# One hybrid block on one core: the splits of the output projection's rows go through a ring of two slots, wider evictions of the values, decay scans and linear-attention groups placed later

## The chip, the cores and the metric

The kernel runs on one core of a Trainium2 chip. The core has a matrix engine (PE, TensorE, with its weight loads shown as PEld), a vector engine (DVE), a scalar engine (ACT), a general engine (POOL, GpSimd) and a queue for transfers (SP), each with an instruction stream of its own that it works off in order. Weights and activations come from DRAM into the on-chip memory SBUF, matmuls write to the banks of PSUM, and DVE or ACT empty these. The metric is the device time of one execution in microseconds (us), as the median of the runs. Lower is better.

## The reference

One block over x with 1024 tokens (T) of width 1024 (D), in float32:

```
h = rmsnorm(x) ; z = h @ w_in      # columns split among three mixers
pool: trailing means over 2, 4, 8, 16 tokens minus u, 64-wide linear per group
gla:  4 heads of 64, chunks of 64: b = cumsum(log_sigmoid(a) / 16) in a chunk
      o = (q e^(b-ref)) (k e^(ref-b))^T v  [causal]  +  (q e^b) S
      S = e^(b_last) S + (k e^(b_last-b))^T v ; rmsnorm per head, times silu(g)
fox:  8 heads of 64, F = cumsum(log_sigmoid(f)), softmax(q k^T / 8 + F_t - F_s) v
y = x + concat(pool, gla, fox) @ w_o
y = y + (silu(rms(y) w_gate) * (rms(y) w_up)) @ w_down ; final rmsnorm
```

Float32 accuracy of products is reached by splitting: each operand is a rounded high part and a low part (value minus high part), and a product is three matmuls, high by high, high by low and low by high.

## The kernel before

The kernel first normalizes x by blocks of 128 tokens, turns them (`norm_T`) to hT in high and low parts, and meanwhile multiplies by the columns for the values of linear attention and the small logits (`psg`). Then follow, in program order: the decays, the inputs of the pool mixer (`pool_in`), linear attention in two pairs of heads A and B (class `Gla`), forgetting attention (values in `fox_values`, queries and keys in `fox_qk`, four pairs of heads in `fox_attend`), the output projection, and the FFN.

*Projections.* `project` loads a column block of the weights, splits it (ACT the high part, DVE or POOL the low part, lines 118 and 119) and runs 48 matmuls of 128x512: two halves of the tokens, each into one of the two PSUM banks "gm" (zgk0p, zgq0p and zgg0p are the banks of keys, queries and gate of pair A, with a 1 for pair B; zp0p and zp1p those of the pool mixer's u; zq.p and zk.p those of attention). ACT or DVE empty a bank into gk, gq, sg or u, and the next but one half can begin only when its bank is empty. Between the matmuls of a projection, PE works through small groups that the call hands over (the lists `smalls`): `turn_keys` (transposes, banks pk), `state` (pkv), `within` (pat), `outputs` (po) and `turned` (pot). These depend on the decay factors d, eq and bc, which POOL, ACT and DVE make from two scans (la into bc).

*Splits of w_o.* `keep_wo(k)` loads block k of w_o (128 rows), splits it into high and low part and stores both in a scratch tensor in DRAM (`wod`), from where the output projection fetches them much later. Before, its eight calls stand behind `fox_values(0)`, with raw, high and low part each in a general slot G. Its rows are wos0 to wos7, with r, h and l behind.

*Memory.* G slots are 33 general tiles of 128x1024, handed out in the order in which they came free. Beside them are rings of the same tiles: "fb" has two slots, used by the squares of the norm (n1sq) and later by the forget sums of a pair of heads, "pp" three and "p" six. A new tile of a ring waits until all use of the slot's last tile is over.

*Values.* `fox_values(q)` makes the values of two pairs of heads for eight token blocks. Each block leaves a bank psv of 128x256, which ACT (high part, line 528) and DVE (low part, 529) empty, once for each of the two pairs of heads.

*Order.* The program is recorded in its order and then put in another by a scheduler of the compiler, which works with times it estimates itself. So where a row stands on an engine is taken from the built program.

Of the kernel before, what the change touches and what calls it, by code (L numbers as in the profile page):

```python
# [18 lines left out]
P = 128  # L19
# [12 lines left out]
def tile_hybrid_block(ctx: ExitStack, tc, x, w_fv, w_gv, w_zt, w_o, w_gu, w_down, ln, w_pool, w_a3, chans, b_f, consts, out):  # L32
# [23 lines left out]
    def free(*names):  # L56
        for n in names:
            idle.append(where.pop(n))

    def R(name, dtype=F32, tag="p"):  # L60

        i = rings[tag].pop(0)
        rings[tag].append(i)
        return big.tile([P, 1024], dtype, tag=f"g{i}", name=name)
# [4 lines left out]
    def f(ap):  # L69
        return ap.bitcast(F32)  # L70
# [207 lines left out]

    def keep_wo(k):

        hi, lo = load_g(w_o[k * P:(k + 1) * P, :], f"wos{k}", tag="G")
        SP.dma_start(wod[k, :, 0], f(hi))
        SP.dma_start(wod[k, :, 1], f(lo))
        free(f"wos{k}h", f"wos{k}l")

    def fetch_wo(k):
        hl = G(f"wo{k}h", F32R), G(f"wo{k}l", F32R)
# [9 lines left out]
    reset = G("reset")  # L297
    DVE.memset(reset, 1.0)
    DVE.memset(e3(reset)[:, :, 0:1], 0.0)
    bcs = []  # L300

    def decays():

        las = []
        for j in range(2):
            la = R(f"la{j}")
            for c in range(2):
                csl = slice(c * 512, c * 512 + 512)
                ps = PS("s", f"pla{j}_{c}")
                PE.matmul(ps, wa[:, j * P:(j + 1) * P], aT[0:48, csl], start=True, stop=True)  # L310
                DVE.tensor_scalar(out=la[:, csl], in0=ps, scalar1=ch[:, 2 + j:3 + j], scalar2=None, op0=ALU.add)
            las.append(la)
        lft = R("lft")
        log_sigmoid([(la, la, R(f"lat{j}", tag="pp")) for j, la in enumerate(las)] + [(fx[0:8], fx[0:8], lft[0:8])])
        for j, la in enumerate(las):
            bc = G(f"bc{j}")
            DVE.tensor_tensor_scan(out=bc, data0=reset, data1=la, initial=0.0, op0=ALU.mult, op1=ALU.add)
            bcs.append(bc)
        ones, Fc = R("ones"), R("Fc")
        DVE.memset(ones[0:8], 1.0)  # L320
        DVE.tensor_tensor_scan(out=Fc[0:8], data0=ones[0:8], data1=fx[0:8], initial=0.0, op0=ALU.mult, op1=ALU.add)
        SP.dma_start(Fd, Fc[0:8])
        free("fx")
# [192 lines left out]

    def fox_values(q, smalls=((),) * NT):

        V = [[G(f"v{2 * q + j}_{i}", F32R).rearrange("p (t h s e) -> p t h s e", t=4, h=2, s=2) for i in range(2)] for j in range(2)]
        ws = [load_w(w_fv[:, q, i * 1024:(i + 1) * 1024], f"wfv{q}_{i}", eng=POOL) for i in range(2)]  # L520
        for tb in range(NT):
            ps = PS("gm", f"psv{q}_{tb}")
            woven(ps[:, 0:256], [(tok(hT, k, tb), tuple(w_[:, (k % 4) * 256:(k % 4) * 256 + 256] for w_ in ws[k // 4]))
                                 for k in range(NK)], smalls[tb])
            for j in range(2):
                v_ = V[j][tb // 4][:, tb % 4]
                pv = ps[:, 128 * j:128 * j + 128].rearrange("p (h e) -> p h e", h=2)
                ACT.activation(v_[:, :, 0], pv, AF.Copy)
                DVE.tensor_tensor(out=v_[:, :, 1], in0=pv, in1=f(v_[:, :, 0]), op=ALU.subtract)
        return V  # L530

    def fox_qk(p):
# [16 lines left out]
    def fox_item(p, a, m, ops, fb, V, Y):  # L549
# [44 lines left out]
        for n in range(m + 1):  # L594
# [10 lines left out]
            for b in range(2):  # L605
                kb = 2 * n + b
                o0 = cut * b
                v_ = V[p % 2][kb // 4][:, kb % 4, a]
                ph = pp[:, 256 * b:512 - o0] if b else pp[:, 0:256]
                pl = pp[:, 768:1024 - o0] if b else pp[:, 512:768]  # L610
                both = (o[:, o0:256], v_.rearrange("p s e -> p (s e)"), ph)
                high = (o[0:64, o0:256], v_[:, 0], pl)
                last = kb == 2 * m + 1
                for n_, args in enumerate((high, both) if last else (both, high)):
                    PE.matmul(*args, start=(kb == 0 and n_ == 0), stop=(last and n_ == 1))  # L615
# [41 lines left out]
            gemm(ps, [((t_[:, 0, o0:o0 + P], t_[:, 1, o0:o0 + P]), (wh[:, ns], wl[:, ns])) for t_, (wh, wl) in zip(mixes, ws)])  # L657
            DVE.tensor_tensor(out=x2[:, ns], in0=ps, in1=x2[:, ns], op=ALU.add)

    decays()  # L660
    free("aT", "reset", "wa")
    us = [pool_in(j) for j in range(2)]
    A = Gla(0)
    A.keys()
    A.queries(((), A.turn_keys()))
    pools = pool_tile(1, us[1]), pool_tile(0, us[0])
    A.gates((A.state(), pools[0] + A.within(0)))
    B = Gla(1)
    B.keys((A.within(1) + A.outputs(0), A.outputs(1) + A.turned(0)))
    B.queries((A.turned(1) + pools[1], B.turn_keys()))  # L670
    free("misc")
    B.gates((B.state(), B.within(0)))
    o_ = [B.outputs(0), B.outputs(1)]
    V = fox_values(0, (B.within(1), o_[0][:1], o_[0][1:], o_[1][:1], o_[1][1:] + B.turned(0), B.turned(1), (), ()))
    for k in range(8):
        keep_wo(k)
    ops = fox_qk(0)
    free("gv0", "gv1", "attb0", "attb1")
    for p in range(4):
# [1 line left out]
            last_mix += [G(f"mix7_{g}", F32R).rearrange("p (h t) -> p h t", h=2) for g in range(2)]  # L681
        Y = G(f"y{p}") if p < 3 else None
        fox_attend(p, ops, V, Y)
        done = [f"{n}{p}_{a}" for n in ("q", "k", "kl") for a in range(2)] + [f"v{p}_{i}" for i in range(2)]
        if p == 1:
            V = fox_values(1)
            free(*[done.pop() for _ in range(2)])
        if p < 3:
            ops = fox_qk(p + 1)
        if p == 2:  # L690
# [432 lines left out]
```

## Time and profile before

| | |
|---|---|
| runs | 1179.23, 1176.51, 1177.58 us; median 1177.58 |
| profiled execution | 1175.42 us, span 1173.7 us, mean clock of PE 0.992 |
| instructions in the span | 15953 |
| norm, mixers, values up to attention's first scores | about 0 to 230 us |
| attention, values of the other half | to about 360 us |
| output projection, then FFN from about 520 us | the rest |
| read from HBM, written to HBM | 105.09 MB, 44.34 MB |

The span runs from the first to the last instruction of the execution; the time holds 1.7 us around it. A row of the timeline gives start and duration of an instruction (or of some alike, "x4", from the first start to the last end), its engine, line, operation, what it writes and reads, and in brackets how long the engine was idle before and what released it. Matmuls overlap, so their starts, and not their durations, show the pace. A row of a DMA issue ends with the time from issue to landing.

### The profile page before, as it was taken

The numbers are of one execution on the slowest core, as the hardware profiler recorded it, in microseconds if no ns is written. First come the engines' busy times: TensorE is split into PE (matmuls) and PEld (weight loads), VectorE is DVE, ScalarE is ACT, GpSimd is POOL, SyncE is SP. The second block draws the span as 40 slices with busy tenths as digits, with TensorE's granted clock in tenths as the row PEclk, the third lists the DMA queues.
The fourth block names the chain that finished last, engine by engine and source line by source line (L and its number), as shares of the span: only waits on it lengthen the run. The fifth ranks groups of instructions, "written<-read, shape, count | busy, mean of one in ns | idle before, by whom it ended". The sixth has DMA issues, their size and how long they took to land.

```text
span 1173.7 us, 15953 instructions
## 1 busy us (share of the span) xinstructions
PE 1136.0 (97%) x5928; PEld 958.5 (82%) x5928; DVE 828.2 (71%) x1365; ACT 536.0 (46%) x970; POOL 340.4 (29%) x260
## 2 busy tenths in 40 slices
PE   6999998999999999998999999999999999999996
PEld 5877878889978888886888888888888888888875
DVE  6697364387746866579997767767686685876686
ACT  6454233466654644456453433444344344334345
POOL 2231123343322413210302221022201370660784
PEclk9999999999999999999999999999999999999999
DMA  7121184411203734431323332242314688333233
GB/s 250 37 73 52 59 295 174 176 39 35 91 18 126 305 132 159 173 112 46 117 86 129 101 115 88 101 134 82 135 54 152 224 322 293 103 95 102 86 112 143
DMA packets 57692, 150.45 MB, mean 128 GB/s; under 512 B 5080, under 2 KB 5512, under 8 KB 57616
## 3 DMA queue, kind: packets, MB, share of 16 engines
q1 hardware_dynamic: 57184, 147.87, 36.5%
q0 software_dynamic: 432, 1.57, 0.4%
q8 instruction: 46, 0.75, 0.3%
q14 instruction: 30, 0.25, 0.1%
HBM read 105.09 MB, written 44.34 MB: 127 GB/s over the span
## 4 chain that ended last, share of the span: by engine, by line
PE 76%; DVE 4%; DMA 1%; issue 1%; POOL 1%; ACT 1%; SPq 0%; POOLq 0%; DVEq 0%; ACTq 0%
PE m L774 36%; PE d L1030 15%; PE pxa L144 4%; PE pxb L144 3%; PE o L615 3%; PE pt L601 2%; PE psv L152 2%; PE s L575 1%; PE s L576 1%; PE zq3p L152 1%; PE zq0p L152 1%; PE zq2p L152 1%; PE zk1p L152 1%; PE zk2p L152 1%; PE zk0p L152 1%
## 5 line engine op out<-in xcount | busy, mean ns | idle before, releaser
L774 PE MATMUL m<-hA_0h,wr 128*128 128x512 f32 x616 | 214.7, 391 | 1.2 <-ACT hr L729 1.2
L774 PE MATMUL m<-hA_1h,wr 128*128 128x512 f32 x616 | 214.9, 389 | 0.0
L774 PEld LDWEIGHTS m<-hA_0h,wr 128*128 128x128 f32 x616 | 116.1, 189 | 25.8 <-ACT hr L729 1.6
L774 PEld LDWEIGHTS m<-hA_1h,wr 128*128 128x128 f32 x616 | 115.8, 188 | 24.2
L1030 PE MATMUL d<-lw,ha 128*128 128x512 f32 x308 | 119.9, 389 | 0.9 <-DVE lw L880 0.9
L774 PE MATMUL m<-hA_0l,wr 128*128 128x512 f32 x308 | 120.3, 391 | 0.0
L774 PE MATMUL m<-hA_1l,wr 128*128 128x512 f32 x308 | 119.9, 389 | 0.0
L1030 PE MATMUL d<-hw,ha 128*128 128x512 f32 x308 | 119.3, 389 | 0.0
L1030 PE MATMUL d<-hw,la 128*128 128x512 f32 x308 | 118.4, 389 | 0.0
L756 ACT ACTIVATE wr<-ws 128x512 fp32r<-128x512 f32 x110 | 69.5, 632 | 101.5 <-DVE ws L755 50.1
L826 POOL TENSOR_TENSOR cg<-cu,cu 128x512 f32<-128x512 f32 x11 | 19.7, 1795 | 302.8 <-DVE cu L803 266.7
L757 DVE TENSOR_TENSOR wr<-ws,wr 128x512 fp32r<-128x512 f32 x110 | 76.8, 704 | 20.6 <-ACT wr L756 20.5
L880 DVE TENSOR_TENSOR la<-ra,ha 128x1024 fp32r<-128x1024 f32 (+1 forms) x42 | 57.2, 1368 | 32.0 <-ACT ha L879 24.7
L590 POOL TENSOR_TENSOR pb<-pb,rl 128x128 f32<-128x128 f32 (+3 forms) x32 | 39.0, 1222 | 117.5 <-DVE rl L587 108.9
L872 POOL TENSOR_TENSOR rw<-wd,wd 128x512 f32<-128x512 f32 x33 | 59.0, 1815 | 47.7 <-PE d L1030 47.6
L879 ACT ACTIVATE ha<-ra 128x1024 fp32r<-128x1024 f32 (+1 forms) x42 | 41.3, 987 | 65.6 <-DMA ra<-cd 56.8
L1030 PEld LDWEIGHTS d<-lw,ha 128*128 128x128 f32 x308 | 57.8, 188 | 13.3 <-DVE lw L880 1.3
L604 DVE TENSOR_TENSOR pp<-pt,pp 128x512 fp32r<-128x512 f32 (+1 forms) x80 | 50.2, 631 | 25.7 <-ACT pp L603 25.3
L774 PEld LDWEIGHTS m<-hA_0l,wr 128*128 128x128 f32 x308 | 58.1, 189 | 12.0
L774 PEld LDWEIGHTS m<-hA_1l,wr 128*128 128x128 f32 x308 | 58.0, 188 | 12.0
L1030 PEld LDWEIGHTS d<-hw,la 128*128 128x128 f32 x308 | 57.8, 188 | 12.1
L1030 PEld LDWEIGHTS d<-hw,ha 128*128 128x128 f32 x308 | 57.8, 188 | 11.9
(398 smaller groups left out, 2690.6 us busy)
## 6 DMA issues: line engine op xcount, KB each, us to landing
ra<-cd SPq DMA_DIRECT2D x35, 512.0 KB, 3.9
wu<-in_w_gu_dram SPq DMA_DIRECT2D x22, 512.0 KB, 4.6
wg<-in_w_gu_dram SPq DMA_DIRECT2D x22, 512.0 KB, 3.7
wd<-in_w_down_dram SPq DMA_DIRECT2D x22, 512.0 KB, 6.4
mix<-mixs SPq DMA_DIRECT2D x14, 512.0 KB, 5.3
cd<-cg SPq DMA_DIRECT2D x11, 512.0 KB, 6.3
cd<-cs SPq DMA_DIRECT2D x11, 512.0 KB, 3.4
cd<-cu SPq DMA_DIRECT2D x11, 512.0 KB, 3.3
```

The source lines that it names most:

```text
L144: PE.matmul(ps, a, b, start=(n == 0), stop=(n == last))
L152: PE.matmul(ps, a, b, start=(i == 0 and n == 0), stop=(i == len(terms) - 1 and n == 2))
L590: POOL.tensor_tensor(out=pb[:, 0:W], in0=pb[:, 0:W], in1=rl[:, 0:1].broadcast_to([P, W]), op=ALU.mult)
L604: DVE.tensor_tensor(out=pp[:, 512:512 + w], in0=pt[:, 0:w], in1=f(pp[:, 0:w]), op=ALU.subtract)
L615: PE.matmul(*args, start=(kb == 0 and n_ == 0), stop=(last and n_ == 1))
L756: ACT.activation(hi, src, AF.Copy)
L757: DVE.tensor_tensor(out=lo, in0=src, in1=f(hi), op=ALU.subtract)
L774: PE.matmul(ps, a, b, start=(n == 0), stop=(n == 11))
L872: POOL.tensor_tensor(out=raw_[:, j * 512:j * 512 + 512], in0=wd[h0, j0 + j][:, e0, :], in1=wd[h1, j0 + j][:, e1, :], op=op)
L879: ACT.activation(hi[:, sl], src, AF.Copy)
L880: DVE.tensor_tensor(out=lo[:, sl], in0=src, in1=f(hi[:, sl]), op=ALU.subtract)
L1030: PE.matmul(banks[t], a[:, o], b[:, ns], start=(j0 + j == 0 and m == 0), stop=(j0 + j == NF // 2 - 1 and m == 2))
```

## The change

`keep_wo` takes two slots of the ring "fb", one for the raw block and one for its high part; the low part is made in place over the raw block. Its eight calls now stand in pairs between the projections of linear attention. The decays are made in three pieces (`decay_logits`, `decay_sums` for each pair, `forget_sums`), the second pair's and the forget sums' later than before. The groups of linear attention are handed to a later projection each. `fox_values` keeps the values of both pairs of heads of two token blocks in one tile, and empties a bank with one ACT and one DVE operation.

```
     def keep_wo(k):
 
-        hi, lo = load_g(w_o[k * P:(k + 1) * P, :], f"wos{k}", tag="G")
+        raw, hi = R(f"wos{k}", tag="fb"), R(f"wosh{k}", F32R, tag="fb")
+        SP.dma_start(raw, w_o[k * P:(k + 1) * P, :])
+        ACT.activation(hi, raw, AF.Copy)
+        DVE.tensor_tensor(out=raw, in0=raw, in1=f(hi), op=ALU.subtract)
         SP.dma_start(wod[k, :, 0], f(hi))
-        SP.dma_start(wod[k, :, 1], f(lo))
-        free(f"wos{k}h", f"wos{k}l")
+        SP.dma_start(wod[k, :, 1], raw)
 
...
-    bcs = []
-
-    def decays():
-
-        las = []
+    las, bcs = [], []
+
+    def decay_logits():
         for j in range(2):
-            la = R(f"la{j}")
+            la = G(f"la{j}")
             for c in range(2):
...
             las.append(la)
-        lft = R("lft")
-        log_sigmoid([(la, la, R(f"lat{j}", tag="pp")) for j, la in enumerate(las)] + [(fx[0:8], fx[0:8], lft[0:8])])
-        for j, la in enumerate(las):
-            bc = G(f"bc{j}")
-            DVE.tensor_tensor_scan(out=bc, data0=reset, data1=la, initial=0.0, op0=ALU.mult, op1=ALU.add)
-            bcs.append(bc)
-        ones, Fc = R("ones"), R("Fc")
+
+    def decay_sums(j):
+
+        la = las[j]
+        log_sigmoid([(la, la, R(f"lat{j}", tag="pp"))])
+        bc = G(f"bc{j}")
+        DVE.tensor_tensor_scan(out=bc, data0=reset, data1=la, initial=0.0, op0=ALU.mult, op1=ALU.add)
+        bcs.append(bc)
+        free(f"la{j}")
+
+    def forget_sums():
+        lft, ones, Fc = (R(n, tag="pp") for n in ("lft", "ones", "Fc"))
+        log_sigmoid([(fx[0:8], fx[0:8], lft[0:8])])
         DVE.memset(ones[0:8], 1.0)
         DVE.tensor_tensor_scan(out=Fc[0:8], data0=ones[0:8], data1=fx[0:8], initial=0.0, op0=ALU.mult, op1=ALU.add)
         SP.dma_start(Fd, Fc[0:8])
...
 
     def fox_values(q, smalls=((),) * NT):
 
-        V = [[G(f"v{2 * q + j}_{i}", F32R).rearrange("p (t h s e) -> p t h s e", t=4, h=2, s=2) for i in range(2)] for j in range(2)]
+        V = [G(f"v{q}_{i}", F32R).rearrange("p (t j h s e) -> p t j h s e", t=2, j=2, h=2, s=2) for i in range(4)]
         ws = [load_w(w_fv[:, q, i * 1024:(i + 1) * 1024], f"wfv{q}_{i}", eng=POOL) for i in range(2)]
         for tb in range(NT):
             ps = PS("gm", f"psv{q}_{tb}")
...
-            for j in range(2):
-                v_ = V[j][tb // 4][:, tb % 4]
-                pv = ps[:, 128 * j:128 * j + 128].rearrange("p (h e) -> p h e", h=2)
-                ACT.activation(v_[:, :, 0], pv, AF.Copy)
-                DVE.tensor_tensor(out=v_[:, :, 1], in0=pv, in1=f(v_[:, :, 0]), op=ALU.subtract)
+            v_ = V[tb // 2][:, tb % 2]
+            pv = ps[:, 0:256].rearrange("p (j h e) -> p j h e", j=2, h=2)
+            ACT.activation(v_[:, :, :, 0], pv, AF.Copy)
+            DVE.tensor_tensor(out=v_[:, :, :, 1], in0=pv, in1=f(v_[:, :, :, 0]), op=ALU.subtract)
         return V
 
     def fox_qk(p):
...
             for b in range(2):
                 kb = 2 * n + b
                 o0 = cut * b
-                v_ = V[p % 2][kb // 4][:, kb % 4, a]
+                v_ = V[kb // 2][:, kb % 2, p % 2, a]
...
-    decays()
-    free("aT", "reset", "wa")
+    decay_logits()
+    decay_sums(0)
+    free("aT", "wa")
     us = [pool_in(j) for j in range(2)]
     A = Gla(0)
     A.keys()
-    A.queries(((), A.turn_keys()))
+    A.queries()
+    decay_sums(1)
+    free("reset")
     pools = pool_tile(1, us[1]), pool_tile(0, us[0])
-    A.gates((A.state(), pools[0] + A.within(0)))
+    A.gates((A.turn_keys(), A.state()))
+    keep_wo(0)
+    keep_wo(1)
+    forget_sums()
     B = Gla(1)
-    B.keys((A.within(1) + A.outputs(0), A.outputs(1) + A.turned(0)))
-    B.queries((A.turned(1) + pools[1], B.turn_keys()))
+    B.keys((A.within(0) + pools[0], A.within(1) + A.outputs(0)))
+    keep_wo(2)
+    keep_wo(3)
+    B.queries((A.outputs(1) + A.turned(0), A.turned(1) + pools[1]))
     free("misc")
-    B.gates((B.state(), B.within(0)))
+    keep_wo(4)
+    keep_wo(5)
+    B.gates((B.turn_keys(), B.state()))
+    keep_wo(6)
+    keep_wo(7)
     o_ = [B.outputs(0), B.outputs(1)]
-    V = fox_values(0, (B.within(1), o_[0][:1], o_[0][1:], o_[1][:1], o_[1][1:] + B.turned(0), B.turned(1), (), ()))
-    for k in range(8):
-        keep_wo(k)
+    V = fox_values(0, (B.within(0), B.within(1), o_[0][:1], o_[0][1:], o_[1][:1], o_[1][1:] + B.turned(0), B.turned(1), ()))
     ops = fox_qk(0)
     free("gv0", "gv1", "attb0", "attb1")
     for p in range(4):
...
             last_mix += [G(f"mix7_{g}", F32R).rearrange("p (h t) -> p h t", h=2) for g in range(2)]
         Y = G(f"y{p}") if p < 3 else None
         fox_attend(p, ops, V, Y)
-        done = [f"{n}{p}_{a}" for n in ("q", "k", "kl") for a in range(2)] + [f"v{p}_{i}" for i in range(2)]
+        done = [f"{n}{p}_{a}" for n in ("q", "k", "kl") for a in range(2)] + [f"v{p // 2}_{i}" for i in range(4) if p % 2]
         if p == 1:
             V = fox_values(1)
-            free(*[done.pop() for _ in range(2)])
+            free(*[done.pop() for _ in range(4)])
         if p < 3:
             ops = fox_qk(p + 1)
         if p == 2:
```

Where the rows of the built program stand is shown at three places. In them wos_ and wosh_ with a number are the raw (later low) and the high part of a block of w_o; 1094, 1101, 1263, 1270, 1405, 1412, 1538 and 1545 are the eight raw blocks in turn.

The first place is ACT in the first pair of linear attention, around the evictions of its keys gk and queries gq; d, dec, eq and bc are decay factors. Before:

```order
L341 ACTIVATE d_0_828<-d_0_828 128x1024
L336 ACTIVATE dec_1127<-bc_700 128x16
L342 ACTIVATE eq_829<-d_0_827 128x1024
L344 ACTIVATE bc_698<-bc_698 128x1024
L343 ACTIVATE d_0_827<-d_0_827 128x1024
L341 ACTIVATE d_1_1130<-d_1_1130 128x1024
L350 ACTIVATE gk_836<-zgk0p_843 128x512
L118 ACTIVATE zgg0h<-zgg0r 128x1024
L350 ACTIVATE gk_836<-zgk0p_869 128x512
L358 ACTIVATE gq_898<-zgq0p_905 128x512
```

And now:

```order
L283 ACTIVATE wosh_1406<-wos_1405 128x1024
L356 ACTIVATE gk_819<-zgk0p_826 128x512
L347 ACTIVATE d_0_811<-d_0_811 128x1024
L342 ACTIVATE dec_1118<-bc_949 128x16
L348 ACTIVATE eq_812<-d_0_810 128x1024
L350 ACTIVATE bc_688<-bc_688 128x1024
L349 ACTIVATE d_0_810<-d_0_810 128x1024
L347 ACTIVATE d_1_1121<-d_1_1121 128x1024
L118 ACTIVATE zgg0h<-zgg0r 128x1024
L356 ACTIVATE gk_819<-zgk0p_852 128x512
L283 ACTIVATE wosh_1413<-wos_1412 128x1024
L364 ACTIVATE gq_881<-zgq0p_888 128x512
```

The evictions of gk and gq now stand behind two copies of w_o blocks, and more of the decays' exponentials stand between the two halves of gk.

On SP's queue, which issues the transfers, the same stretch reads now:

```order
L282 DMA wos_1270<-in_w_o_dram 128x1024
L285 DMA wod<-wosh_1271 128x1024
L286 DMA wod<-wos_1270 128x1024
L282 DMA wos_1405<-in_w_o_dram 128x1024
L117 DMA zgk1r<-in_w_zt_dram 128x1024
L285 DMA wod<-wosh_1406 128x1024
L328 DMA Fd<-Fc 8x1024
L286 DMA wod<-wos_1405 128x1024
L282 DMA wos_1412<-in_w_o_dram 128x1024
L117 DMA zgq1r<-in_w_zt_dram 128x1024
```

Loads and stores of the blocks (to wod) stand between the loads of the projections' weights; before, the eight blocks' transfers came behind the loads of all weights of linear attention.

The second place is DVE at the end of the values of the first half; psv are the value banks, v the values, gy and on belong to linear attention's pair B, q to attention. Before:

```order
L529 TENSOR_TENSOR v_1_1511<-psv_5_1761,v_1_1511 128x2x64
L274 TENSOR_TENSOR gy_1390<-gy_1390,mh_1792 128x1024
L119 TENSOR_TENSOR wos5l<-wos5r,wos5h 128x1024
L529 TENSOR_TENSOR v_1_1509<-psv_6_1801,v_1_1509 128x2x64
L119 TENSOR_TENSOR wos1l<-wos1r,wos1h 128x1024
L529 TENSOR_TENSOR v_1_1511<-psv_6_1801,v_1_1511 128x2x64
L529 TENSOR_TENSOR v_1_1509<-psv_7_1830,v_1_1509 128x2x64
L529 TENSOR_TENSOR v_1_1511<-psv_7_1830,v_1_1511 128x2x64
L119 TENSOR_TENSOR wos4l<-wos4r,wos4h 128x1024
L539 SCALAR_TENSOR_TENSOR q_0_1923<-zq0p_1935,q_0_1923 64x512
```

And now:

```order
L93 TENSOR_SCALAR gn_v<-gss_1806 128x8
L473 SCALAR_TENSOR_TENSOR gy_1420<-pot_0_1826,ch,sg_1419 128x512
L534 TENSOR_TENSOR v_2_1554<-psv_5_1778,v_2_1554 128x4x64
L462 TENSOR_TENSOR on_1_1803<-po_1_0_1762,gn_r 128x4x64
L462 TENSOR_TENSOR on_1_1803<-po_1_1_1763,gn_r 128x4x64
L534 TENSOR_TENSOR v_3_1555<-psv_6_1834,v_3_1555 128x4x64
L473 SCALAR_TENSOR_TENSOR gy_1420<-pot_1_1859,ch,sg_1419 128x512
L534 TENSOR_TENSOR v_3_1555<-psv_7_1872,v_3_1555 128x4x64
L274 TENSOR_TENSOR gy_1420<-gy_1420,mh_1865 128x1024
L544 SCALAR_TENSOR_TENSOR q_0_1899<-zq0p_1911,q_0_1899 64x512
```

The low parts of w_o are gone from there, a bank has one v row, and the last groups of linear attention stand between the banks.

The third place is DVE at the end of attention's pair 1; pp are softmax parts, k and kl the keys of pair 2 from the bank zk2p, y the output of pair 1. Before:

```order
L604 TENSOR_TENSOR pp_1_3_2_3133<-pt_1_3_2_3132,pp_1_3_2_3133 128x512
L604 TENSOR_TENSOR pp_1_3_3_3145<-pt_1_3_3_3144,pp_1_3_3_3145 128x384
L544 TENSOR_TENSOR kl_0_3410<-zk2p_3482,k_0_3408 64x512
L544 TENSOR_TENSOR kl_0_3410<-zk2p_3515,k_0_3408 64x512
L621 TENSOR_TENSOR y_2685<-o_1_3_3107,ot_1_3_3155 64x256
L544 TENSOR_TENSOR kl_1_3411<-zk2p_3482,k_1_3409 64x512
L544 TENSOR_TENSOR kl_1_3411<-zk2p_3515,k_1_3409 64x512
L274 TENSOR_TENSOR y_2685<-y_2685,mh_3548 128x1024
```

And now:

```order
L609 TENSOR_TENSOR pp_1_3_2_3109<-pt_1_3_2_3108,pp_1_3_2_3109 128x512
L609 TENSOR_TENSOR pp_1_3_3_3121<-pt_1_3_3_3120,pp_1_3_3_3121 128x384
L626 TENSOR_TENSOR y_2661<-o_1_3_3083,ot_1_3_3131 64x256
L549 TENSOR_TENSOR kl_0_3370<-zk2p_3442,k_0_3368 64x512
L549 TENSOR_TENSOR kl_0_3370<-zk2p_3475,k_0_3368 64x512
L274 TENSOR_TENSOR y_2661<-y_2661,mh_3508 128x1024
L549 TENSOR_TENSOR kl_1_3371<-zk2p_3442,k_1_3369 64x512
L549 TENSOR_TENSOR kl_1_3371<-zk2p_3475,k_1_3369 64x512
```

The rows of y moved ahead: its sum ahead of all of kl, its split (line 274) ahead of the second head's.

## Prediction

> **What bounds the kernel now.** I read the page first, for the engine that sets the end.
>
> ```profile
> PE 1136.0 (97%) x5928; PEld 958.5 (82%) x5928; DVE 828.2 (71%) x1365; ACT 536.0 (46%) x970; POOL 340.4 (29%) x260
> ```
>
> PE is busy for 97% of the span. So an edit is worth what it takes from PE's idle time, or what it adds there. The number and the shapes of the matmuls don't change. From the FFN on, the built program's order is the same as before, so I ask for PE's waits only where the order differs, from 60 to 360 us.
>
> ```profile
> PE zq0p L152 <- DVE v L529: 3.5, 1, 3.5
> PE zq3p L152 <- DVE kl L544: 2.5, 1, 2.5
> PE pk L375 <- DVE d L351: 2.1, 1, 2.1
> PE psv L152 <- DVE v L529: 1.5, 1, 1.5
> PE o L615 <- DVE pp L604: 0.7, 2, 0.3
> PE pot L466 <- DVE on L456: 0.4, 1, 0.4
> ```
>
> Each row gives the total, the number of waits and the longest. All that the change can remove there is about 10 us. To this comes the granted clock, which a view by stretches shows (the clock stands third from the end, behind the busy times).
>
> ```profile
> 95.60:101.00 5.40, 5.37 (x28) 4.50 (x29) 4.48 (x5) 0.88 (x1) 1.95 (x1) 1.00 0.27 92
> 176.20:179.70 3.50, 3.50 (x19) 3.50 (x18) 0.42 (x2) 0.00 (x0) 1.64 (x1) 0.51 0.12 48
> 203.50:206.90 3.40, 3.40 (x10) 2.62 (x9) 0.00 (x0) 0.00 (x0) 1.07 (x1) 0.51 0.99 294
> ```
>
> After the 2.1 us wait of pk the clock stayed at 1.00. After the waits of psv and zq0p it was 0.51 for one stretch of about 3.4 us each, in which PE was busy throughout: 3.45 x 0.49, 1.7 us lost each time.
>
> **Gains: the eight splits of w_o leave the stage of the values.** The timeline shows why psv and zq0p wait.
>
> ```profile
> 172.15 1.06 ACT L118 ACTIVATE wos6h<-wos6r 128x1024 fp32r<-128x1024 f32 x1 [7.61 <-DMA wos6r<-in_w_o_dram]
> ...
> 175.44 0.36 PE L152 MATMUL psv<-wfv_0h,hT 128*128 128x256 f32 x1 [1.54 <-DVE v L529]
> ...
> 198.91 2.35 POOL L119 TENSOR_TENSOR zq0l<-zq0r,zq0h 128x1024 fp32r<-128x1024 f32 x1 [7.11 <-issue]
> 199.75 2.58 DVE L119 TENSOR_TENSOR wos1l<-wos1r,wos1h 128x1024 fp32r<-128x1024 f32 x1 [1.77 <-ACT wos1h L118]
> ...
> 202.59 0.74 PE L152 MATMUL zq0p<-hT,zq0h 128*128 128x512 f32 x2 [3.48 <-DVE v L529]
> ```
>
> In the first case ACT holds the copy of a value bank behind wos6h, which waits 7.61 us for its load. In the second DVE holds it behind wos1l, which takes 2.58 us beside POOL's zq0l. With the splits gone, both causes go. The wider evictions alone would not do it: the operation ahead was what was long. What is late next at zq0p is its own low part: its load now waits for a slot, and zq0l still takes 2.35 us on POOL, of which I leave 0.8 in front of PE (0 to 3.5: the whole wait). So the gains are 1.54 (psv), 0.40 (pot), 3.48 - 0.8 (zq0p) and 2 x 1.7 of clock. The wait of pk goes as well, 2.07, because turn_keys now comes a projection later. The sum is 10.1 us. The halving of 16 evictions to 8 on two engines that are not the bound counts nothing beyond this; the matmuls of psv are the cover. The woven groups that come later are the same matmuls in other gaps; the last of them now stand in the seventh of eight value blocks, and what they feed (the mixes' stores) is read only by the output projection, so I count 0 for them too, as for the forget sums, which attention reads after the values.
>
> **Costs: the ring's turn.** Raw and high part take both slots, so a block's load must wait until the low part of the block before has landed in DRAM. Load and stores never overlap. Two views of the DMA queue have the durations.
>
> ```profile
> zgk1r<-in_w_zt_dram SPq DMA_DIRECT2D x1, 512.0 KB, 3.6
> ```
>
> ```profile
> wod<-wos6l SPq DMA_DIRECT2D x1, 512.0 KB, 2.6
> ...
> wod<-wos5l SPq DMA_DIRECT2D x1, 512.0 KB, 4.7
> ```
>
> A load alone takes 3.6 us (zgk1r at 70 us, of the same size). The store of a low part takes 2.6 to 4.7; early on there is less traffic than at 4.7, and I take 3.1. ACT's copy is the 1.06 of wos6h above, and DVE's difference 1.23, as for y in the last fence below. A turn is 3.6 + 1.06 + 1.23 + 3.1 and 0.2 for the handovers, 9.2 us. With the shortest store and no handovers it is 8.5; with the longest store, 10.8. The first load starts when the slots, which hold norm tiles, come free.
>
> ```profile
> 41.35 0.29 PE L144 MATMUL psg<-wgv2l,hT 128*128 128x280 f32 x1
> 41.48 0.29 PE L144 MATMUL psg<-wgv2h,hT 128*128 128x280 f32 x1
> 41.60 0.60 PE L180 MATMUL n1t<-ident,n1sq 128*128 128x128 f32 x4
> ```
>
> The transposes in the last row, which end at 42.2, are the last readers of the slot. In the new order they stand ahead of 24 psg matmuls. These start 0.13 apart, 3.1 in all, so with 0.3 to issue it the first load goes out at 39.4. The fourth goes out three turns later at 67.0 and lands at 70.6.
>
> **Place A, the keys.** In the new order ACT does the copy of that fourth block ahead of the log sigmoid of the decays, and the decays' scans, differences and exponentials follow. Three engines' rows from before, each in its own view:
>
> ```profile
> 71.14 2.29 DVE L317 TENSOR_TENSOR_SCAN bc<-reset,la 128x1024 f32<-128x1024 f32 x1
> 73.35 1.20 DVE L256 SCALAR_TENSOR_TENSOR la<-la,lat 128x1024 f32<-128x1024 f32 x1
> 74.58 3.87 DVE L317 TENSOR_TENSOR_SCAN bc<-reset,la 128x1024 f32<-128x1024 f32 x1
> ```
>
> ```profile
> 73.54 0.61 PE L152 MATMUL zgk0p<-hT,zgk0h 128*128 128x512 f32 x2
> ...
> 84.65 0.73 PE L152 MATMUL zgq0p<-hT,zgq0h 128*128 128x512 f32 x2
> ...
> 114.86 0.73 PE L152 MATMUL zgk1p<-hT,zgk1h 128*128 128x512 f32 x2
> ```
>
> ```profile
> 85.45 0.58 ACT L350 ACTIVATE gk<-zgk0p 128x512 f32<-128x512 f32 x1
> ...
> 116.41 1.28 ACT L368 ACT_TABLE_LOAD   x1
> ```
>
> The first scan took 2.29 us, the second 3.87 beside POOL's work on d; a POOL operation alone took 1.95 (in the stretch from 95.60 above), so the two hold each other up and I add them one after the other. ACT's copy ends at 71.7, four exp and ln of 1.05 at 75.9, la at 77.1, the first scan at 79.4; POOL 81.4, zgq0l on DVE 82.6, POOL 84.5, the second scan 86.8, an add of the pool mixer 88.0, POOL 89.9. Behind that last POOL result ACT's queue has an exp (91.0), zgg0h (92.1) and only then the copy of gk's second half (0.58), which ends at 92.8 with the handovers. A projection takes 11.1 us (73.54 to 84.65), half of one 5.5, so PE needs that bank at 90.1 for the second half of zgq0p. **New wait: 2.7 us** (0 to 4). Before, nothing late stood ahead of gk's copies.
>
> **Place B, the queries.** DVE's queue has the low part of the fifth block behind the scan of the forget sums. That scan follows POOL's 89.9 and ends at 92.2, the low part at 93.4; store 96.5, next load 100.1, ACT's copy 101.2. Right behind it in ACT's queue stands the copy of gq's first half, done at 101.8. PE is ready for zgg0p two projections and A's wait after 73.5, at 98.4. **New wait: 3.4 us** (0 to 6).
>
> **Place C, the gate.** The second half of sg stands behind the eighth block's copy, a further weight copy and a table load (1.28 above). That block lands two turns after 100.1, at 118.5, and about 2.4 later for two mixer operations of 1.2 ahead of the low parts on DVE. With 2 x 1.06, 1.28 and 0.6 the bank is free at 124.9. PE began zgk1p at 114.86; without the old wait (2.07) and some 1.8 of woven work that has moved on, and with 6.1 for A and B, it begins at 117.1, and needs the bank after half a projection and 0.7 of woven matmuls, at 123.3. **New wait: 1.6 us** (0 to 3.4). A to C make 7.7.
>
> **Place D, the end of pair 1.** The order of DVE changes there too. Its rows from before:
>
> ```profile
> 350.69 1.28 DVE L544 TENSOR_TENSOR kl<-zk2p,k 64x512 fp32r<-64x512 f32 x2 [0.61 <-PE o L615]
> 352.00 0.42 DVE L621 TENSOR_TENSOR y<-o,ot 64x256 f32<-64x256 f32 x1
> 352.45 1.30 DVE L544 TENSOR_TENSOR kl<-zk2p,k 64x512 fp32r<-64x512 f32 x2
> 353.78 1.23 DVE L274 TENSOR_TENSOR y<-y,mh 128x1024 f32<-128x1024 f32 x1
> ```
>
> zq3p waits for the first kl of the third row. Before, y's split (the last row, which waits for mh, an ACT copy of 1.06) stood behind it; now the 0.42 and the split stand ahead. From the last output matmul the chain is ACT's ot (0.38), 0.42, 1.28, 1.23 and 0.65 (one kl), 3.96, and 0.5 for mh and handovers: 4.45 us, where the wait was 2.5. Three matmuls of scores that PE still has cover 0.35, so 1.55 more; and 0.45 for short waits such as that of o above, which lose their fillers. **2.0 us** (0 to 3.5).
>
> **The clock.** The new waits at A to C lie between 128x512 matmuls, as the 2.07 us wait did that cost no clock. I take 0, and 3.4 (two stretches) as the other end. The rows do not say which gap trips it: 1.54 us did, 2.07 us did not. The Trainium skill ("TensorE: Matmul & The Clock Gate", section "HAM oscillation — how this bites in real kernels") puts the rule abstractly as no idle gaps of PE over about 3.4 us; by it none of the gaps here but B's, at its limit, would cost clock, and the sum would be the same. The trace disagrees with it as a bound: a gap of 1.54 us was followed by 3.5 us at 0.51.
>
> **The sum** against the profiled execution (1175.42 us): -10.1 + 7.7 + 2.0 = -0.4, so 1175.0. The median of the runs is 1177.58, 2.2 above that execution; the same difference put on it gives **1177.2**. SP's queue also waits in the ring's turns, with zgk1r, zgq1r and zgg1r behind it; each of these is wanted a projection (11 us) after its place, longer than a turn, so I count 0. The other cover is at zgk0p's second half, which PE begins at 79.0: the bank's emptying follows the exp and ln of 75.9, a weight copy (1.06) and itself (0.6), 77.6. These 1.4 us of slack are used up if a turn is 0.5 longer.
>
> **The rivals.**
> 1. *Faster: the ring keeps ahead.* By the chains above each 0.1 us of a turn moves A by 0.3, B by 0.1 (four turns there, three in PE's own delay) and C by 0.2, 0.6 in all. With a turn of 8.0 instead of 9.2, A's 2.7 and C's 1.6 are gone and B keeps 1.3 (its chain ends 4.8 earlier, at 97.0, PE is ready at 95.7). Then -10.1 + 1.3 + 2.0 = -6.8, **1170.8**; with a lower D some two less. For it: the DMA queue has little to do from 40 to 70, and 2.6 is a measured store. Against: 8.5 was the least that the rows give.
> 2. *Slower: longer turns.* The same 0.6 for each 0.1 us, upwards. It decides from a turn of 9.3, where A to C outweigh the gains less D; above 9.7 it costs over 0.2%. At 10.3 the sum is -0.4 + 6.6, **1183.8**. For it: 4.7 is a measured store, and the weights of the projections load in the same stretch. Against: there are fewer other loads than at 160 to 200.
> 3. *The values' wait stays.* If zq0l comes as late as before, zq0p keeps 3.5 instead of 0.8 and its slow stretch: +4.4, **1181.6**. For it: the same 2.35 on POOL; against: the 7.11 of idle time on POOL ahead of it.
>
> **How the numbers follow.** Chances: the forecast 0.38, rival 1 0.32, rival 2 0.22, rival 3 0.08. About 0.2%, or 2.4 us, is what a measurement of this kernel can tell from no change. So faster 0.32, same 0.38, slower 0.30. The forecast's own range is 1175 to 1180, from a turn of 8.9 to one of 9.7. The whole range goes from just below rival 1 to just past rival 2, **1169.5 to 1184.0**; the ends of D, the clock and zq0p move it by 2 to 4 inside that, and only several of them together leave it.
>
> **What would show it.** In the profile after, the waits of psv, pot and pk should be gone, zq0p's about 0.8, and the clock full from 170 to 210. New PE waits should stand at zgq0p (released by ACT gk), zgg0p (ACT gq) and zgk1p (ACT sg), 1.5 to 3.5 us each, and zq3p's should be 4 to 5. ACT's wosh operations should wait for their loads about 9 us apart. I am wrong if wosh never waits on its DMA there, if the turn is under 8.5 or over 10, or if PE waits in the stage of the values as before.

## The result, and the profile after

The changed kernel takes **1187.48 us** (median of 4 runs, 1185.13 to 1189.73), the kernel before 1177.1 us beside it: a ratio of 1.0091, 95% interval [1.0078, 1.0105]. It is slower by 0.9%, some 10 us. The prediction was 1177.2 with a range to 1184.0, so the time lies outside it, by 3.5 us. The profiled execution took 1185.13 us, 9.7 more than that of before.

Where the time goes is read best from when the same work starts in the two traces (the view by tile gives first and last start of each matmul group; times in us).

| PE starts | before | after | difference |
|---|---|---|---|
| first matmul of zgk0p (keys, pair A) | 73.5 | 71.8 | -1.7 |
| first of zgg0p (gate, pair A) | 98.8 | 103.8 | +5.0 |
| first of zgg1p (gate, pair B) | 148.4 | 153.3 | +4.9 |
| first of zq0p (attention) | 202.6 | 202.6 | 0.0 |
| last of zk1p | 258.8 | 258.1 | -0.7 |
| first of zq3p | 353.2 | 354.4 | +1.2 |
| last of s (scores) | 464.4 | 464.8 | +0.4 |
| last of pxb (output projection) | 530.9 | 541.0 | +10.1 |

So in the stretch about which the prediction argued the change costs little on balance: 0.0 us at zq0p, 1.2 at zq3p. Most of the loss arises behind it, in the output projection, which the prediction had not looked at. From 427 us to the last pxb PE is idle for 7.3 us, against 0.2 before. The other 3 of the 10 us stand at 427 us as work that is still left (from there to the last pxb PE is busy for 107.0 us, before for 104.0), so they were lost ahead of it. The table of the time before ends attention at about 360 us; its last output matmul starts at 492.6 us, and the output projection's matmuls are woven in from 396.8 us on. PE's waits in the changed kernel, first in the stretch of the prediction (60 to 360 us), then behind it (425 to 560 us), show both; a row has the total, the number and the longest.

```profile
PE zgq0p L152 <- ACT gk L356: 8.5, 1, 8.5
PE zq3p L152 <- DVE kl L549: 2.2, 1, 2.2
PE s L580 <- POOL k L551: 1.8, 1, 1.8
PE pt L606 <- DVE pp L609: 0.7, 1, 0.7
PE zq0p L152 <- DVE v L534: 0.5, 1, 0.5
```

```profile
PE n2pt L742 <- DVE n2sq L737: 3.5, 1, 3.5
PE pxb L144 <- DMA mix<-mixs: 2.8, 1, 2.8
PE pxa L144 <- DMA mix<-mixs: 1.8, 1, 1.8
PE pxb L144 <- DMA wo5h<-wod: 1.0, 1, 1.0
...
PE pxb L144 <- DMA wo4l<-wod: 0.7, 1, 0.7
```

The waits of psv, pot and pk are gone, and that of zq0p is 0.5. One wait, 8.5 us at zgq0p, has taken their place. Behind 425 us the changed kernel waits for mixes and weights four times, 6.3 us. The kernel before has one such wait there:

```profile
PE pxb L144 <- DMA wo6h<-wod: 0.2, 1, 0.2
```

**The 8.5 us at zgq0p** come from POOL. PE waits there until ACT has copied the second half of the keys (gk), and that copy stands in ACT's queue behind exponentials that wait for POOL's d:

```profile
88.51 1.06 ACT L347 ACTIVATE d<-d 128x1024 f32<-128x1024 f32 x1 [8.86 <-POOL d L345]
...
96.19 0.58 ACT L356 ACTIVATE gk<-zgk0p 128x512 f32<-128x512 f32 x1
```

POOL's rows and those of DVE in the changed kernel:

```profile
78.03 10.45 POOL L345 TENSOR_TENSOR d<-bc 128x1024 f32<-128x1024 f32 x1 [41.24 <-DVE bc L319]
88.44 2.91 POOL L346 TENSOR_TENSOR d<-bc 128x1024 f32<-128x1024 f32 x1
```

```profile
75.66 2.28 DVE L319 TENSOR_TENSOR_SCAN bc<-reset,la 128x1024 f32<-128x1024 f32 x1
78.10 0.91 DVE L326 MEMSET ones<- 8x1024 f32 x1
78.94 1.15 DVE L119 TENSOR_TENSOR zgq0l<-zgq0r,zgq0h 128x1024 fp32r<-128x1024 f32 x1
80.02 2.27 DVE L319 TENSOR_TENSOR_SCAN bc<-reset,la 128x1024 f32<-128x1024 f32 x1
82.21 1.19 DVE L495 TENSOR_TENSOR pa<-u 128x1023 f32<-128x1023 f32 x1
83.33 2.27 DVE L327 TENSOR_TENSOR_SCAN Fc<-ones,fx 8x1024 f32<-8x1024 f32 x1
85.53 1.19 DVE L284 TENSOR_TENSOR wos<-wos,wosh 128x1024 f32<-128x1024 f32 x1
86.65 0.13 DVE L494 COPY pa<-u 128x1 f32<-128x1 f32 x1
86.71 2.84 DVE L495 TENSOR_TENSOR pa<-u 128x1023 f32<-128x1023 f32 x1
```

POOL's first d starts right behind the first scan and takes 10.45 us where the work needs 1.95. In that time DVE runs six operations of 0.9 to 2.3 us, the five with two inputs each at its duration alone. Only the one at 86.71 is drawn out (2.84 for 1.2), and POOL's first d ends 1.8 us into it, so that is where POOL seems to work at last. In the trace of before the same two engines took turns, one operation each (DVE 3.87, 2.89, 2.91):

```profile
73.51 2.79 POOL L339 TENSOR_TENSOR d<-bc 128x1024 f32<-128x1024 f32 x1 [23.07 <-DVE bc L317]
76.26 3.92 POOL L340 TENSOR_TENSOR d<-bc 128x1024 f32<-128x1024 f32 x1
80.14 2.87 POOL L339 TENSOR_TENSOR d<-bc 128x1024 f32<-128x1024 f32 x1
```

The Trainium skill ("SBUF — State Buffer", section "SBUF: two separate sides") says that a DVE operation with two SBUF inputs and a GpSimd operation that reads SBUF share a pair of ports as an exclusive lock, which whichever starts first holds for the whole instruction. The trace agrees that they exclude each other. It does not show that the first to start gets in: POOL's row starts at 78.03, ahead of all six rows of DVE, and POOL lets them pass; whether a row's start is the moment at which it asks for the ports, the trace doesn't say.

**The waits in the output projection** come from late loads. SP's rows in the kernel before, and then in the changed one, for the low and high parts of w_o that the second half of the projection needs (wo4 to wo7):

```profile
429.94 0.33 SPq L289 DMA_DIRECT2D wo4h<-wod  x1
430.62 0.33 SPq L289 DMA_DIRECT2D wo4l<-wod  x1
...
434.48 0.32 SPq L289 DMA_DIRECT2D wo5h<-wod  x1
...
466.08 0.33 SPq L289 DMA_DIRECT2D wo5l<-wod  x1
```

```profile
433.35 0.38 SPq L291 DMA_DIRECT2D wo4h<-wod  x1
...
471.80 0.33 SPq L291 DMA_DIRECT2D wo7h<-wod  x1
472.18 0.42 SPq L291 DMA_DIRECT2D wo4l<-wod  x1
472.72 0.35 SPq L291 DMA_DIRECT2D wo5h<-wod  x1
...
476.28 0.32 SPq L291 DMA_DIRECT2D wo6h<-wod  x1
476.91 0.53 SPq L652 DMA_DIRECT2D mix<-mixs  x1
```

Before, three of the eight were loaded at 430 to 434 and five at 466. Now one is loaded at 433 and seven at 472 to 476, in one burst with a mix behind it, and PE needs the first of them at once. The reason lies in the slots. G slots are given out in the order in which they came free. Before, pair 2's two value tiles came free after pair 2. In the change the four tiles of a half serve both of its pairs, and come free only after the second one. After pair 2 the queue of free slots is two shorter than before, so each tile behind takes a slot that comes free later. Followed through the program's order, wo4l takes the slot of a mix of the first half of the tokens before (mix2_0), and in the change that of a mix of the second half (mix0_1), which the projection still reads until about 472 us (the last pxa matmul with wo0h starts at 471.6, and wo4l's load goes out at 472.18).

### The profile page after: what moved, and what is told of

Its sections match the earlier page's. It is cut to its first block, busy times and chain, and to the rows that moved or that the text cites. A ratio compares the mean times of both kernels' runs of the same rounds, so it can differ in the third digit from the quotient of the medians.

```text
span 1183.4 us, 15914 instructions
## 1 busy us (share of the span) xinstructions
PE 1135.5 (96%) x5928; PEld 956.9 (81%) x5928; DVE 823.4 (70%) x1349; ACT 534.2 (45%) x956; POOL 346.2 (29%) x260
## 4 chain that ended last, share of the span: by engine, by line
PE 62%; DMA 3%; DVE 3%; issue 1%; POOL 1%; ACT 0%; POOLq 0%; DVEq 0%; ACTq 0%
PE m L789 35%; PE d L1045 15%; PE pxa L144 3%; PE pxb L144 3%; DMA mix<-mixs 2%; PE zq3p L152 1%; PE pt L606 1%; PE o L620 1%; PE zk3p L152 1%; DMA wo5h<-wod 1%; PE n2pt L742 1%; PE s L581 1%; PE s L580 1%; DVE hs L916 0%; POOL f_r L107 0%
## 5 line engine op out<-in xcount | busy, mean ns | idle before, releaser
L887 POOL TENSOR_TENSOR rw<-wd,wd 128x512 f32<-128x512 f32 x33 | 60.9, 1874 | 46.7 <-PE d L1045 46.6
L589 ACT ACTIVATE pb<-pb,mn 128x128 f32<-128x128 f32 (+3 forms) x64 | 49.4, 773 | 52.8 <-DVE mn L585 52.2
```

The lines of the kernel that those rows point to most:

```text
L589: ACT.activation(pb[:, 0:W], pb[:, 0:W], AF.Exp, bias=mn[:, 0:1], scale=-1.0, accum_out=l[:, i:i + 1])
L887: POOL.tensor_tensor(out=raw_[:, j * 512:j * 512 + 512], in0=wd[h0, j0 + j][:, e0, :], in1=wd[h1, j0 + j][:, e1, :], op=op)
```

## The experiments

The theory on the output projection is V: the value tiles' late release. The theory on zgq0p is that POOL's d is held up. The first rival of each is the other: either could be the loss. Ratios are against runs of the kernel before on the same chip; each is estimated over the runs with its 95% interval, and need not be the quotient of the two medians.

**Values as before, the rest of the change kept.** The old `fox_values`, its index in `fox_item`, and the old frees:

```
-        V = [G(f"v{q}_{i}", F32R)... for i in range(4)]
+        V = [[G(f"v{2 * q + j}_{i}", F32R)... for i in range(2)] for j in range(2)]
...
-        done = [...] + [f"v{p // 2}_{i}" for i in range(4) if p % 2]
+        done = [...] + [f"v{p}_{i}" for i in range(2)]
```

> The changed kernel with the values as before: tiles for each pair of heads, two evictions per bank and engine, pair 2's tiles free after pair 2. Theory V (the shared value tiles of pairs 2 and 3 are freed only after pair 3, so wo4l, wo5h and others load late and in one burst): PE's waits for wo and mix in 440 to 545 us (7.1 us in the changed kernel) go, the time falls by 7 to 10 us, to about 1178, level with before within 0.2%. Rival P (POOL's held-up d and the 8.5 us wait at zgq0p are the loss): those waits are untouched, so the time stays at 1186 to 1188.

Measured: 1175.91 us, ratio 0.9998 [0.9987, 1.0009]. The whole loss is gone, as V has it. PE still waits 8.1 us at zgq0p, so that wait isn't the loss: the rest of the change pays for it. Busy time in 427 to 535 us, first number behind the length, for before, changed, and this kernel:

```profile
427.00:535.00 108.00, 106.93 (x586) 91.29 (x585) 73.68 (x127) 55.76 (x116) 22.54 (x27) 1.00 0.45 156
```

```profile
427.00:535.00 108.00, 100.71 (x553) 85.41 (x552) 66.54 (x118) 48.79 (x100) 20.10 (x25) 1.00 0.43 152
```

```profile
427.00:535.00 108.00, 106.89 (x586) 91.43 (x585) 73.74 (x126) 56.55 (x117) 22.50 (x27) 1.00 0.44 158
```

PE was idle for 1.1, 7.3 and 1.1 us of that stretch. (By the rows above the waits for wo and mix in the changed kernel are 6.3 us, not the 7.1 of the expectation.) The loads are back in their old places, too: wo4h, wo4l and wo5h go out at 429 to 434 us, the other five at 465 to 467.

**The kernel before, pair 2's value tiles held longer.** One line:

```
-        done = [...] + [f"v{p}_{i}" for i in range(2)]
+        done = [...] + [f"v{v}_{i}" for v in ((0,), (1,), (), (2, 3))[p] for i in range(2)]
```

> The kernel before, with one line changed: pair 2's two value tiles are freed with pair 3's, nothing else; evictions, splits and decays as before. Theory V: waits for wo and mix of 6 to 9 us appear in 440 to 545 us, and the time rises to 1184 to 1187. Rival W (the loss there comes from the wide evictions or the ring, not from when the tiles come free): no such waits, 1176 to 1178.

Measured: 1180.15 us against 1176.08, ratio 1.0031 [1.0013, 1.005]. Nothing but the moment of a release is changed in the program (the scheduler's order follows from it: PE's differs from 436 us on), and 4.1 us are lost, with waits for wo5h (1.4) and wo4l (0.9). That is about half of what V expected. One of the eight loads goes out at 435 us and seven at 469 to 473. The change holds pair 0's tiles longer as well, which this kernel doesn't.

**Both halves' tiles held.** The same line with `((), (0, 1), (), (2, 3))[p]`, and four frees instead of two after pair 1:

> The kernel before with the value tiles of both halves freed only after their second pair, as the shared tiles are: pair 0's with pair 1's, pair 2's with pair 3's; evictions narrow. The second experiment, which held pair 2's alone, gave +3.6 us. Theory V in full (only when tiles come free): now the whole loss of the value part, 8 to 11 us, to 1184 to 1187. Rival W (the wide evictions' own order of work has a share of about 6): still about 1180.

Measured: 1184.21 us against 1176.15, ratio 1.0073 [1.0056, 1.0089]: 8.1 us, with evictions, splits and decays as before. V in full holds. The loads of wo go out as in the changed kernel, one at 434 us and seven at 473 to 477, and PE is busy for 103.25 us of 427 to 535:

```profile
427.00:535.00 108.00, 103.25 (x567) 87.42 (x566) 66.58 (x119) 49.71 (x102) 21.05 (x27) 1.00 0.43 156
```

That is 4.8 us idle, 3.7 more than before. Another 2.1 are lost up to the end of pair 1, where zq3p starts at 355.3 instead of 353.2, and where a wait of 1.8 at s for POOL's k appears in this kernel as in the changed one. The other 2.3 are not placed.

**The value part of the change alone**, in the kernel before:

> The kernel before with the whole value part of the change alone: shared tiles of two token blocks, one eviction of 128x256 per bank and engine, both halves' tiles free after the second pair. Theory V (only the late release counts): the same as with narrow evictions and tiles held, 1184.2, a ratio of 1.006 to 1.009. Rival W (the wider evictions add to the loss or take from it): more than 2.4 us away from that, below 1181.8 or above 1186.6.

Measured: 1185.01 us against 1175.18, ratio 1.008 [1.006, 1.01]. That can't be told from the narrow evictions with held tiles (1.0073), and the loads of wo go out in the same way, one at 433 us and seven at 470 to 474. So the width of the evictions is worth nothing that a run shows, and the layout that allows it costs 8 to 10 us.

**No memset behind the first scan.** What decides how long POOL waits? In the changed kernel a memset of ones came first behind the scan.

```
+    ones = cst.tile([P, 1], F32, name="ones")
+    DVE.memset(ones, 1.0)
...
-        lft, ones, Fc = (R(n, tag="pp") for n in ("lft", "ones", "Fc"))
+        lft, Fc = (R(n, tag="pp") for n in ("lft", "Fc"))
...
-        DVE.memset(ones[0:8], 1.0)
-        DVE.tensor_tensor_scan(out=Fc[0:8], data0=ones[0:8], ...)
+        DVE.tensor_tensor_scan(out=Fc[0:8], data0=ones[0:8, 0:1].broadcast_to([8, T]), ...)
```

> The changed kernel with the 8x1024 memset of ones, which stood on DVE right behind the first scan, replaced by a column of ones made at the start and read broadcast; the forget scan then follows the first scan on DVE. Theory M (the memset took the port ahead of POOL): POOL's first d takes 2 to 4 us instead of 10.45, the wait at zgq0p falls from 8.5 to under 3, the time by 5 to 9 us. Theory B (POOL gets in only where DVE's row of operations breaks off, whatever comes first): d still takes 9 to 10 us, the wait 7 to 8.5, the time within 1.5 us of the changed kernel. Fair turns, as the prediction had it: d takes about 4.3 us and the wait is 3 to 4.

Measured: 1183.09 us against 1176.08, ratio 1.0067 [1.0041, 1.0093]; the wait at zgq0p is 6.4.

```profile
77.34 4.97 POOL L346 TENSOR_TENSOR d<-bc 128x1024 f32<-128x1024 f32 x1 [41.43 <-DVE bc L321]
82.27 6.23 POOL L347 TENSOR_TENSOR d<-bc 128x1024 f32<-128x1024 f32 x1
```

No theory fits. The first d waited for two operations of DVE, the second for three; together they end at 88.5 instead of 91.3. So the memset isn't the whole cause, and turns are not fair either.

**A small POOL operation ahead of d** (128x1, from la):

```
+            POOL.tensor_tensor(out=warm[:, 0:1], in0=la[:, 0:1], in1=la[:, 1:2], op=ALU.subtract)
```

> The changed kernel with one 128x1 operation on POOL added, some 2 us ahead of its first d; every other row stands as it did. Theory C (POOL starts slowly after 41 us without work): the small operation takes the slow start, d takes 2 to 4 us and the wait at zgq0p falls below 4. Theories M and B: d takes about 10.4 us as before and the wait stays at 8 to 9.

One run: 1185.74 us. The small operation took 0.19 us at 73.56, d again 10.45, the wait is 8.3. A slow start of POOL is out.

**A short copy on DVE behind zgq0l:**

```
+            DVE.tensor_copy(la[:, 0:1], la[:, 0:1])
```

> The changed kernel with a 128x1 copy in place on DVE right behind zgq0l, two operations behind the first scan; it also moves the second scan behind the forget scan. Theory G (POOL gets the port where DVE has a short one-input operation): the first d ends there and takes about 4 us instead of 10.45, and the wait at zgq0p falls by 2 to 5 us. Rival N (it gets in only after the whole row of operations): d takes 10 us again.

One run: 1183.95 us. The copy ran at 80.34 for 0.13 us, and d still took 9.33; POOL got in at 85.9, behind three more operations of DVE. Theory G falls, though the wait at zgq0p is 6.7 here, 1.8 less. When POOL gets the ports is left open: in these kernels it waited for one to six operations of DVE, and neither the memset nor a short copy decided it.

**Values and decays as before, ring and groups kept.** The first kernel with the decays in one piece again, ahead of linear attention:

```
-    decay_logits()
-    decay_sums(0)
+    decays()
...
-    decay_sums(1)
...
-    forget_sums()
```

> The first experiment's kernel (values as before) with the decays as before too: all three scans at one place ahead of linear attention, so that POOL's first d comes while DVE still has a dependent pair of operations. What is left of the change is the ring, the places of the splits and the groups. Theory (POOL's late d makes the 8.1 us wait at zgq0p): d takes 3 to 4 us each, that wait falls to 0 to 2, and the time by 5 to 8 us to 1168 to 1171, a ratio of 0.993 to 0.996. Rival R (the ring's turns are due a wait in any case, at the next bank): a wait of 3 or more turns up at zgq0p, zgg0p or zgk1p, and the time stays within 2.4 us of before.

Measured: **1171.71 us** against 1176.15, ratio 0.9957 [0.9941, 0.9972]. It is faster than both kernels. The wait at zgq0p is gone; others come a projection later (2.4 and 2.3 at pkv), so the gain, 4.4 us, is just short of the 5 to 8 that were expected. PE's waits in 60 to 360 us and POOL's first d in this kernel:

```profile
PE zq3p L152 <- DVE kl L546: 2.5, 1, 2.5
PE pkv L395 <- ACT k2t L378: 2.4, 1, 2.4
PE pkv L395 <- DVE St L399: 2.3, 2, 1.5
PE zq0p L152 <- POOL zq0l L119: 1.3, 1, 1.3
```

```profile
73.24 2.79 POOL L341 TENSOR_TENSOR d<-bc 128x1024 f32<-128x1024 f32 x1 [23.74 <-DVE bc L319]
75.99 3.92 POOL L342 TENSOR_TENSOR d<-bc 128x1024 f32<-128x1024 f32 x1
```

Against the first experiment (0.9998) it says what the split decays cost beside the ring and the groups: about 0.4%, 4 to 5 us. They were not run alone.

**The groups alone**, in the kernel before:

> The kernel before with only the groups of linear attention handed to the later projections; splits, values and decays as before. By the prediction's sum the wait of pk (2.07) goes and those of psv and zq0p stay: 1174 to 1176, or within 0.2% if another group waits instead. Rival: the groups that now stand in the values' stage wait there behind the splits, +1 to +3.

Measured: 1172.29 us against 1176.15, ratio 0.997 [0.996, 0.9979]. More than was expected: not only pk's wait goes but psv's too, and zq0p's falls to 1.8; a new one of 2.7 at zgg0p (released by ACT's gq) gives some back.

**The ring and the new places of the splits alone**, in the kernel before:

> The kernel before with only the splits of w_o changed: the ring of two slots and the eight calls in pairs between the projections of linear attention; values, decays and groups as before. By the prediction the waits of psv, pot and zq0p with their two stretches of half clock go (8.0 us), and the ring's turns give some back at the banks of keys, queries and gate: with the decays early the wait at zgq0p is under 2, and the sum is -4 to -8, 1168 to 1172. Rival: the ring's waits on ACT come at another bank and take it all, within 2.4 us of 1176.

Measured: 1172.32 us against 1175.18, ratio 0.9973 [0.9956, 0.9991]. The gain, 2.9 us, is less than the 4 to 8 that were expected; the ten runs lie between 1168.8 and 1176.6, and the trace is of one with 1170.79. The waits of psv and pot are gone, and zq0p's is 1.1. The ring's turns put no wait of 2 us or more at the banks of keys, queries and gate; its rows of waits in 60 to 360 us:

```profile
PE zq3p L152 <- DVE kl L546: 2.5, 1, 2.5
PE pk L377 <- DVE d L353: 1.9, 1, 1.9
PE zq0p L152 <- DVE v L531: 1.1, 1, 1.1
```

**State of pair A a projection later**, on top of the fastest kernel:

```
-    A.gates((A.turn_keys(), A.state()))
+    A.gates((A.turn_keys(), pools[0]))
-    B.keys((A.within(0) + pools[0], A.within(1) + A.outputs(0)))
+    B.keys((A.state() + A.within(0), A.within(1) + A.outputs(0)))
```

> The fifth experiment's kernel (ring and groups kept, values and decays as before) with two groups exchanged: the state of pair A goes a projection later, a pool group takes its place. There PE waited 4.7 us at pkv for the turned keys and the state. Theory: these waits go and nothing as long takes their place, 1167 to 1170, a ratio of 0.991 to 0.995 against before. Rival: the groups behind the state wait for it in turn (pat or po), 1171 to 1174.

Measured: 1173.1 us against 1175.43, ratio 0.9984 [0.9975, 0.9992]: not better than the fastest. One wait of 3.9 at pkv stands where three stood (4.7 in all), and the clock goes to half behind it (0.50 from 122 to 128 us, in the kernel without the exchange 1.00). The time is that of the rival, but the groups behind the state hardly wait (0.2 at po).

## Why the prediction was wrong, point by point

- **The step that failed** is in its first part: "From the FFN on, the built program's order is the same as before, so I ask for PE's waits only where the order differs, from 60 to 360 us". The order differs further on, too: only from 583 us of the trace of before are PE's matmuls in the same order in both, and the stretch that was left out holds most of the loss. With it goes the sentence that the halving of the evictions "counts nothing beyond this": the evictions count nothing, but the tiles that they need are held for one pair longer. A term of +8 to +10 us for slots was missing from the sum (the values alone 1.008, the release alone 1.0073).
- **What was looked at came out nearly as summed.** As far as zq0p's start the sum is -2.07 (pk) - 1.54 (psv) - 0.40 (pot) - 2.7 (zq0p) - 1.7 (clock) + 7.7 (A to C) = -0.7; measured 0.0. From there to zq3p's start it is -1.7 (clock) + 2.0 (D) = 0.3; measured 1.2. That the first sum came out is in part luck: A cost three times what was taken, B and C nothing, the clock behind A 1.5 us that the sum had at 0, and the first matmul of zgk0p came 1.7 us earlier, which the sum didn't have.
- **By parts** the ratio is 0.9957 for ring and groups, 0.9998 with the split decays, 1.0091 with the values: the forecast of no change (-0.4 us) fits the change without its value part, and the value part is what the sum lacked.
- **The gains were right.** The waits of pk, psv and pot are gone, zq0p's is 0.5 for 0.8, and the clock is full from 170 to 210 us.
- **The ring's turn was right at first**: loads go out at 37.5, 46.7, 55.4 and 65.9 us, turns of 8.7 to 10.5 for the 9.2 taken, and the fifth at 74.3. The next two turns take 15.1 and 16.8 us, because a low part waits in DVE's row (the fifth block's from 79.2 to 85.5) and a copy in ACT's; the last takes 10.0. So the prediction's own sign of being wrong, a turn of over 10, turned up.
- **Place A was mis-sized, 2.7 for 8.5.** The prediction let POOL and DVE take turns by one operation. POOL's first d waited for six. B and C were wrong with it: they are 0. In the trace PE begins zgg0p at 103.8, 5.6 us after gq's first copy has ended, so the delay at A seems to cover them; with the decays early, where there is no wait at A, they are 0 as well. The three together are 8.5 for 7.7, and 1.5 us of half clock behind A that the sum had at 0:

```profile
93.00:96.40 3.40, 0.00 (x0) 0.00 (x0) 0.09 (x1) 3.40 (x5) 1.24 (x1) 0.50 0.00 0
96.40:99.80 3.40, 2.99 (x7) 2.41 (x8) 3.40 (x5) 1.79 (x3) 0.00 (x0) 0.50 0.36 36
```

- **Place D** was right in sum, +1.9 from zk1p's end to zq3p's start for 2.0, but not in its rows: zq3p's wait is 2.2 for 4 to 5 (before 2.5), and two other waits (s for POOL's k 1.8, pt 0.7) are new. So the sum came out by luck. The kernel with both halves' tiles held shows the wait at s, 1.8, without any other part of the change, so it too comes from the tiles; pt's 0.7 stands only in the kernels with the shared tiles, that of the value part alone among them. The clock, which the sum left alone here, was 0.62 from 356.6 to 360.0 us, for 0.92 before.
- **The rivals.** Rival 2 had the direction but not the mechanism, a turn over 9.7: turns of 15 and 17 came, but in the kernel with the ring alone, which is faster than before, one of 18.3 (70.7 to 89.1) makes no bank of keys, queries or gate wait. A rival on the slots, "tiles shared by two pairs come free later, and loads behind them wait", was missing, though the changed lines on `done` and `free` say it.

## What to carry to other kernels

When a change makes a tile live longer, follow the slot to its next owners, however far behind, and look at the load that fills it: here two slots of each half, held for one pair longer, cost 8 us, a good part of it in loads of the output projection that the change doesn't touch. A part of a change that runs show to gain (ring and groups, 0.3% each alone, 0.4% together) can be buried by another part, so parts are worth measuring one at a time. A wait can also be paid for by work that runs anyway: the split decays, with 8 us at zgq0p, cost about half of that, since later waits shrank.

## What the runs showed of the hardware

A POOL operation of 1.95 us on 128x1024 took up to 10.45 us beside a row of two-input operations of DVE, and 2.8 to 3.9 where both took turns; neither an earlier POOL operation nor a short copy on DVE changed the long case much (10.45 and 9.33). The wait of 2.1 us at pk cost no clock in the trace of before, nor in the kernel with both halves' tiles held (2.08 us). In the kernel with pair 2's tiles held, 2.07 us at the same place, the clock behind it was 0.50 from 96 to 98 us, and in the kernel with the value part alone, 2.06 us, it was 0.53:

```profile
96.30:99.70 3.40, 3.40 (x12) 2.71 (x11) 2.90 (x4) 0.46 (x1) 1.94 (x1) 0.53 0.03 8
```

So the length of a wait doesn't settle whether half a clock follows; at the same place it came in two traces and not in two others.
